# A hybrid decoder layer on one core: the low parts of the weights, the products with g_mix and the cross query's scaling made by VectorE in place of GpSimd

## The chip, the cores and the metric

The kernel runs on one core of a Trainium2 chip. The core has five engines that run side by side: TensorE (PE in the profile; PEld is its loading of the stationary operand), VectorE (DVE), ScalarE (ACT), GpSimd (POOL), and SyncE (SP), which here issues the DMAs. The metric is the device time of one execution in microseconds (us); lower is better.

## The reference

One layer of a decoder for 512 tokens of width 1024, in float32, and a final norm:

```python
h = _rms_norm(x, g_mix[l])
fq, fk, fv, f_logit, dq, dk, dv, gate_a, gate_b = jnp.split(h @ w_in[l], offsets, axis=-1)
...
merged = (jax.nn.sigmoid(gate_a) * (y_a @ w_branch_a[l])
          + jax.nn.sigmoid(gate_b) * (y_b @ w_branch_b[l]))
x = x + merged @ w_out[l]
x = x + _cross_attention(_rms_norm(x, g_cross[l]), _rms_norm(mem, g_mem[l]),
                         w_cq[l], w_ckv[l], w_co[l])
...
x = x + _hier_moe(hm, w_group[l], b_group[l], w_expert[l], b_expert[l],
                  w_exp_gate[l], w_exp_up[l], w_exp_down[l]).reshape(b, s, d)
return _rms_norm(x, g_final)
```

y_a is a causal attention with a forget gate (8 heads of 64), y_b a differential attention with rotary positions (4 heads). The cross-attention has 4 heads and 256 memory rows. The last part routes each token to 2 of 32 experts, whose weights are some 200 MB of float32.

## The kernel before

The program is one long manual schedule: each engine executes its instructions in the order in which the code issues them, and waits where an operand or a buffer is not ready.

**Split products.** The products with the weights of the first half (w_in, the branch, output and cross projections) are made of three matmuls each: every float32 operand is split into a high part, rounded to the fast matmul type, and a low part, the remainder; high x high, low x high and high x low are summed (mm3, L278 to L280). `split` (L175) makes both parts: ScalarE copies the high part (L176), and another engine subtracts it from the source (L177).

**The stream of weights.** A `Stream` object W holds the list of weight chunks in order of use, 32 of them, each 1024 rows by 256 columns or the same size in another shape, and each handled in two halves of 128 x 1024 elements. For a half, SyncE loads the raw weights into one of three buffers (L141), ScalarE makes the high part wh, and the low part wl is made by GpSimd for the halves in the set `self.pool`, that is 12 to 63 without 57 and 59, and by VectorE for the rest. The raw buffer is loaded anew when both parts are done. `W.more()` splits one half ahead; the main loop calls it once per attention iteration behind `it.combine()`, and twice for the second attention (L950 to L956). Outside that loop `W.use` calls it in front of each unit's matmuls.

**The stages.** First x, transposed, is multiplied by g_mix (h_gain, L326; x itself is normed only later, by a factor per token) and split, one tile of 128 tokens at a time, and the first projection is made (to 30 us of the profile). Then 16 iterations of the first attention (class Fox) and 8 of the second (class Diff) follow, each with one or two projection units (t_unit, rope_unit, gate_unit, branch_unit) between the scores and the product with the values; TensorE works through them in this order: scores, unit, values of the iteration before, transposes of the softmax rows (tf or td). VectorE scales the softmax rows (`combine`: L592 for Fox; L698 and L699 for Diff), then evacuates the unit's bank, then copies the transposed rows (pf L603, pd L711). The banks in PSUM are handed out in turn, and the next scores need the banks of the transposed rows. After the attentions come the last units: gate and branch projections, the latter with four instructions of VectorE (L846, L853, two of L857) around two high parts of ScalarE (L856); the keys and values of the memory; and the output projection (out_unit: wop, L1018). The cross query's weights w_cq are multiplied by g_cross when they have been loaded (`self.scale`, L143), before they are split.

**The experts** follow from about 508 us on: per pair of experts TensorE multiplies with 12 pages of 1 MB each, which SyncE loads into a ring of 15 pages as TensorE uses pages up (EX.used).

Of the kernel before, what the change touches and what calls it, by code (L numbers as in the profile page):

```python
# [10 lines left out]
F32 = mybir.dt.float32  # L11
# [4 lines left out]
OP = mybir.AluOpType  # L16
AX = mybir.AxisListType

P = 128
# [3 lines left out]
KD = D // P  # L23
# [15 lines left out]
def tile_hybrid_block(  # L39
# [5 lines left out]
    V, A, PE, G = nc.vector, nc.scalar, nc.tensor, nc.gpsimd  # L45
# [10 lines left out]
    def page(shape, dt, name):  # L56
        return pgp.tile(list(shape), dt, name=name, tag="pg")
# [3 lines left out]
    def work(shape, dt, name, tag="w"):  # L61
        return wk.tile(list(shape), dt, name=name, tag=tag, bufs=bufs[tag])
# [28 lines left out]
    gm = c1.tile([P, KD], F32, name="gm")  # L91
# [14 lines left out]
    def xT(t, k0=0, n=KD):  # L106
        return XT[t // 2][:, t % 2, k0:k0 + n]
# [8 lines left out]
    class Stream:  # L116
        def __init__(self):
            self.spec, self.raw, self.hl = [], {}, {}
            self.loaded = self.done = self.next = 0
            self.lazy = False  # L120
            self.pool = set(range(12, 64)) - {57, 59}
            self.scale, self.new, self.land, self.ahead = {}, {}, {}, {}

        def add(self, src, k, n):
# [3 lines left out]
        def load(self, upto):  # L128

            while self.loaded < min(upto, 2 * len(self.spec), self.done + self.ahead.get(self.loaded // 2, NLD)):  # L130
                i, j = divmod(self.loaded, 2)
                src, k, n = self.spec[i]
                sl = slice(j * k // 2, (j + 1) * k // 2)
                if i in self.land:
                    if j == 0:
                        self.land[i] = page([P, k, n], F32, f"wr{i}")
                    raw = self.land[i][:, sl]
                else:
                    raw = work([P, k // 2, n], F32, f"wr{i}{j}", "ld")
                self.raw[self.loaded] = raw  # L140
                nc.sync.dma_start(raw, src[:, sl])  # L141
                if i in self.scale:
                    G.tensor_tensor(raw, raw, self.scale[i][:, sl, None].to_broadcast([P, k // 2, n]), op=OP.mult)  # L143
                self.loaded += 1

        def split(self, upto):

            while self.done < min(upto, 2 * len(self.spec)):
                i, j = divmod(self.done, 2)
                self.load(self.done + 1)  # L150
                _, k, n = self.spec[i]
                if j == 0:
                    self.hl[i] = [self.new.get((i, u), page)([P, k, n], F32R, f"w{u}{i}") for u in "hl"]
                hi, lo = self.hl[i]
                sl = slice(j * k // 2, (j + 1) * k // 2)
                n = k // 2 // 2 if self.done < 2 else k // 2
                for k0 in range(0, k // 2, n):
                    d = slice(sl.start + k0, sl.start + k0 + n)
                    split(hi[:, d], lo[:, d], self.raw[self.done][:, k0:k0 + n], G if self.done in self.pool else V)
                self.done += 1  # L160
                self.load(self.done + 4)

# [9 lines left out]

            self.split(self.next)

    def split(hi, lo, src, E=V):  # L175
        A.activation(hi, src, AF.Copy)  # L176
        E.tensor_tensor(lo, src, hi.bitcast(F32), op=OP.subtract)  # L177

    W = Stream()

# [114 lines left out]
    def nat_unit(chunk, t, dst, d0, name, nt=1, tag="a"):  # L295

        wh, wl = W.use(chunk, t // 2)
        o = bank(f"{name}p{t}", tag)
        for i in range(nt):
            sl = slice((t + i) * P, (t + i + 1) * P)  # L300
            gemm(o[:, 256 * i:256 * i + 256], KD, lambda k: hk(HH, k, sl), lambda k: hk(HL, k, sl),
                 lambda k: wh[:, k, :], lambda k: wl[:, k, :])

        def evac():
            for i in range(nt):
                A.activation(dst[:, t + i, d0:d0 + 256], o[:, 256 * i:256 * i + 256], AF.Copy, scale=rT[:, t + i:t + i + 1])

        return evac
# [9 lines left out]
    def h_split(t, qs=(0, 1)):  # L318

        sl = slice(t * P, (t + 1) * P)  # L320
        for q in qs:
            split(HH[q][:, :, sl], HL[q][:, :, sl], xT(t, 4 * q, 4))

    def h_gain(t, E, k0=0, n=KD):
        v = xT(t, k0, n)
        E.tensor_tensor(v, v, gm[:, k0:k0 + n, None].to_broadcast([P, n, P]), op=OP.mult)  # L326

    def h_stat(t):
        rms_stat(xt(t), f"nx{t}", out=rT[:, t:t + 1])
# [5 lines left out]

    W.lazy = True
    lg = c1.tile([P, KD, 16], F32R, name="lg")
    h_gain(0, V, 0, 4)
    h_gain(0, G, 4, 4)
    h_split(0, (0,))  # L340
    W.split(1)
    h_split(0, (1,))
    W.split(2)
    evs = []
    for t in range(NT):
        evs.append(nat_unit(c_fv[0], t, fv, 0, "fv0", tag="as"[t // 2]))
        if t + 1 < NT:
            h_gain(t + 1, G)
            h_split(t + 1)
        if t == 1:  # L350
            split(lg[:, :, 0:8], lg[:, :, 8:16], lg_r)
            W.split(3)
        if t == 2:
            h_stat(0)
            h_stat(1)
            evs.pop(0)()
            evs.pop(0)()
            h_stat(2)
            h_stat(3)
# [185 lines left out]
    class Fox:  # L545
# [60 lines left out]
        def av(self):  # L606
            pr, b = self.pr, self.b
            st = Fox.state[pr]
            if b == 0:
                st["y"] = bank(f"yo{pr}", "y")  # L610
            for j in range(b + 1):
                for i in range(2):
                    h = 2 * pr + i
                    PE.matmul(st["y"][64 * i:64 * i + 64, b * P:(b + 1) * P], fv[:, j, h * 64:h * 64 + 64],
                              self.pt[i][:, j * P:(j + 1) * P], start=(b + j == 0), stop=(j == b),
                              skip_group_check=True)
            if b == NT - 1:
                return lambda: lambda: split(YAH[:, pr, :], YAL[:, pr, :], st["y"])
# [690 lines left out]
    for step in """T0 N0 U20 Q0 U21 K0 T1 N1 U30 U22 W Q1 S0 M0 K1 U23 U31 N2 T2 S1 P0 Q2 M1 U32 A0 U33 K2 T3 O0 N3 S2  # L1309
# [5 lines left out]
        f, t = step[0], int(step[1]) if len(step) > 1 else 0  # L1315
# [244 lines left out]
    for p in range(NE // 2):  # L1560
# [4 lines left out]
        for a in range(2):  # L1565
            e = 2 * p + a
            sl = slice((2 * qi + a) * CAP, (2 * qi + a + 1) * CAP)
# [211 lines left out]
```

## Time and profile before

| | |
|---|---|
| median of 3 runs | 1009.11 us (1008.07 to 1009.96) |
| profiled execution | 1009.81 us, its span 1008.1 us |
| PE busy | 966.5 us (96%) |
| DVE busy | 457.2 us (45%) |
| ACT busy | 308.6 us (31%) |
| POOL busy | 200.3 us (20%), of it 120.6 in 50 low parts (L177) |
| granted TensorE clock, mean | 0.984 |

The profile is of one execution. Its time is a little longer than its span, which runs from the first to the last instruction. Times in the rows below count from the start of the span. Line numbers are those of the kernel before; the changed kernel's are one lower from L121 on. A busy TensorE is not one at its peak: matmuls overlap, and their ends are modelled. The granted clock is 1.00 at 2.4 GHz and 0.50 at 1.2 GHz.

### The profile page before, as it was taken

How to read it: one execution, taken by the hardware profiler on the slowest of the kernel's cores; microseconds unless marked ns; L12 is line 12 of the kernel's file. 1: busy time of each engine (PE TensorE's matmuls, PEld its weight loads, DVE VectorE, ACT ScalarE, POOL GpSimd, SP SyncE). 2: the span in 40 equal slices, each digit the busy share in tenths (PEclk: the TensorE clock that was granted, in tenths of full speed). 3: DMA queues.
4: the chain of work that ended last, by engine and by line, in shares of the span. 5: the costliest groups of instructions: out<-in, count | busy, mean ns of one | idle time of the engine just before them, and what ended most of it. 6: DMA issues, size and time to landing. Idle time of an engine off the chain costs nothing. (4 is left out here: it accounts for less than half of the span.)

```text
span 1008.1 us, 13868 instructions
## 1 busy us (share of the span) xinstructions
PE 966.5 (96%) x5494; PEld 643.8 (64%) x5495; DVE 457.2 (45%) x967; ACT 308.6 (31%) x672; POOL 200.3 (20%) x245
## 2 busy tenths in 40 slices
PE   8999899999989999999799999999999999999985
PEld 7787677787878898998646536364453635436332
DVE  6554885846562526445632333323233332233335
ACT  5344444444353344245321112021121212112104
POOL 4841122223444555410100000000000000000003
PEclk8999999999999999999899999999999999999998
DMA  8221121121131247237389899999999999999902
GB/s 307 85 65 62 63 63 64 43 85 63 63 126 63 84 131 266 84 126 301 159 324 422 330 423 416 423 421 418 421 421 422 420 419 421 420 421 419 411 12 84
DMA packets 47862, 246.19 MB, mean 244 GB/s; under 512 B 4784, under 2 KB 12208, under 8 KB 23728
## 3 DMA queue, kind: packets, MB, share of 16 engines
q1 hardware_dynamic: 47648, 245.24, 61.4%
q8 instruction: 45, 0.74, 0.3%
q14 instruction: 25, 0.20, 0.1%
q10 hardware_dynamic: 144, 0.00, 0.0%
HBM read 243.13 MB, written 2.10 MB: 243 GB/s over the span
## 5 line engine op out<-in xcount | busy, mean ns | idle before, releaser
L1410 PE MATMUL gu<-gu,xg 128*64 128x512 f32 x960 | 210.5, 593 | 1.7 <-PEq L1479 1.6
L1410 PEld LDWEIGHTS gu<-gu,xg 128*64 128x64 f32 x960 | 72.9, 137 | 133.2 <-issue 121.1
L177 POOL TENSOR_TENSOR wl<-wr,wh 128x1024 fp32r<-128x1024 f32 x50 | 120.6, 2419 | 186.5 <-ACT wh L176 179.4
L1432 PE MATMUL yd<-dn,A 128*64 128x512 f32 x472 | 110.4, 596 | 0.0
L1454 DVE TENSOR_TENSOR xr<-cb,xr 128x512 f32<-128x512 f32 x120 | 75.7, 684 | 50.6 <-PE cb L1450 50.4
L1415 DVE SCALAR_TENSOR_TENSOR A<-A,gu 128x256 f32<-128x256 f32 x32 | 13.5, 421 | 176.1 <-ACT A L1414 176.1
L1550 POOL MEMSET A<- 128x128 f32 x1 | 0.2, 206 | 438.2 <-PE pth L275 438.2
L1432 PEld LDWEIGHTS yd<-dn,A 128*64 128x64 f32 x472 | 34.9, 137 | 64.3 <-issue 63.4
L1414 ACT ACTIVATE A<-gu 128x256 f32<-128x256 f32 x32 | 12.3, 385 | 201.2 <-PE gu L1410 201.2
L176 ACT ACTIVATE wh<-wr 128x1024 fp32r<-128x1024 f32 (+1 forms) x66 | 67.1, 1026 | 8.0 <-POOL wr L143 6.8
L1450 PE MATMUL cb<-Y,ohT 128*128 128x512 f32 x240 | 67.5, 412 | 0.9
L1440 DVE SCALAR_TENSOR_TENSOR Y<-yd,ws,Y 128x512 fp32r<-128x512 f32 x32 | 23.9, 750 | 91.8 <-ACT Y L1439 89.9
L1238 PE MATMUL ga<-G,hnh 128*128 128x256 f32 x256 | 64.6, 290 | 0.2 <-DVE ge L1358 0.2
L1238 PE MATMUL ga<-G,hnl 128*128 128x256 f32 x256 | 62.8, 283 | 0.0
L1439 ACT ACTIVATE Y<-yd,ws 128x512 fp32r<-128x512 f32 x32 | 21.9, 687 | 126.8 <-PE yd L1432 126.8
L1450 PEld LDWEIGHTS cb<-Y,ohT 128*128 128x128 f32 x240 | 42.7, 191 | 12.5 <-DVE xr L1454 3.2
L1238 PEld LDWEIGHTS ga<-G,hnh 128*128 128x128 f32 x256 | 48.5, 190 | 3.1 <-issue 2.4
L1238 PEld LDWEIGHTS ga<-G,hnl 128*128 128x128 f32 x256 | 48.6, 190 | 0.6
L1384 ACT ACTIVATE xg<-ga,smc 128x256 f32<-128x256 f32 x64 | 29.8, 475 | 52.3 <-PE ga L1238 52.3
L278 PE MATMUL wop<-wh,mh 128*128 128x256 f32 x128 | 36.9, 288 | 2.9 <-DVE xr L1018 1.8
L279 PE MATMUL wop<-wl,mh 128*128 128x256 f32 x128 | 36.4, 284 | 0.6 <-POOL wl L177 0.6
L280 PE MATMUL wop<-wh,ml 128*128 128x256 f32 x128 | 36.3, 283 | 0.0
(611 smaller groups left out, 1962.6 us busy)
## 6 DMA issues: line engine op xcount, KB each, us to landing
gu<-in_w_gu_dram SPq DMA_DIRECT2D x120, 1024.0 KB, 12.3
dn<-in_w_dn_dram SPq DMA_DIRECT2D x55, 1024.0 KB, 17.4
wr<-in_w_inp_dram SPq DMA_DIRECT2D x40, 512.0 KB, 3.7
Z<-in_w_gu_dram SPq DMA_DIRECT2D x8, 1024.0 KB, 14.8
wr<-in_w_out_dram SPq DMA_DIRECT2D x8, 512.0 KB, 6.5
Z<-in_w_dn_dram SPq DMA_DIRECT2D x4, 1024.0 KB, 19.8
dn<-in_w_dn_dram SPq DMA_DIRECT2D x6, 512.0 KB, 13.8
x<-in_x_dram SPq DMA_DIRECT2D x2, 1024.0 KB, 11.6
```

The costliest lines, as they stand in the source:

```text
L176: A.activation(hi, src, AF.Copy)
L177: E.tensor_tensor(lo, src, hi.bitcast(F32), op=OP.subtract)
L278: PE.matmul(o, lh, rh, start=first, stop=False)
L279: PE.matmul(o, lh, rl, start=False, stop=False)
L280: PE.matmul(o, ll, rh, start=False, stop=last)
L1238: PE.matmul(o, CX[u, t // 2][:, t % 2, kb * P:(kb + 1) * P], GQ[q][:, t].rearrange("p e s -> p (e s)"), start=(first and u == "h"), stop=( ...
L1384: A.activation(XG[q][:, kb], o, AF.Copy, scale=gfc[:, kb:kb + 1])
L1410: PE.matmul(gu[64 * f:64 * f + 64, :], xg(2 * i + j), w[:, :, j, 256 * f:256 * f + 256], start=(i + j == 0), stop=(i + j == 4))
L1432: PE.matmul(y[j][64 * a:64 * a + 64, :], hT[a][:, f % 2, f // 2], w(a, f)[:, j, f % 2], start=(f == 0), stop=(f == 3))
L1440: V.scalar_tensor_tensor(yl[rows, j], y[j][rows], ws, yh[rows, j].bitcast(F32), op0=OP.mult, op1=OP.subtract)
L1450: PE.matmul(banks[j], oh[:, t * P:(t + 1) * P], y[u][:, j], start=(u == 0), stop=(u == 1))
L1454: V.tensor_tensor(xs, banks[j], xs, op=OP.add)
```

## The change

GpSimd makes no low part any more, and no product of x with g_mix, and does not scale the cross query's weights; VectorE does, at the same places of the code. One line moves: the product of the second half of the first token tile, which GpSimd made beside the first half's, now stands behind the first half chunk's split, so that VectorE takes it up there.

```diff
-            self.pool = set(range(12, 64)) - {57, 59}
...
                 if i in self.scale:
-                    G.tensor_tensor(raw, raw, self.scale[i][:, sl, None].to_broadcast([P, k // 2, n]), op=OP.mult)
+                    V.tensor_tensor(raw, raw, self.scale[i][:, sl, None].to_broadcast([P, k // 2, n]), op=OP.mult)
...
-                    split(hi[:, d], lo[:, d], self.raw[self.done][:, k0:k0 + n], G if self.done in self.pool else V)
+                    split(hi[:, d], lo[:, d], self.raw[self.done][:, k0:k0 + n])
...
-    def split(hi, lo, src, E=V):
+    def split(hi, lo, src):
         A.activation(hi, src, AF.Copy)
-        E.tensor_tensor(lo, src, hi.bitcast(F32), op=OP.subtract)
+        V.tensor_tensor(lo, src, hi.bitcast(F32), op=OP.subtract)
...
-    def h_gain(t, E, k0=0, n=KD):
+    def h_gain(t, k0=0, n=KD):
         v = xT(t, k0, n)
-        E.tensor_tensor(v, v, gm[:, k0:k0 + n, None].to_broadcast([P, n, P]), op=OP.mult)
+        V.tensor_tensor(v, v, gm[:, k0:k0 + n, None].to_broadcast([P, n, P]), op=OP.mult)
...
-    h_gain(0, V, 0, 4)
-    h_gain(0, G, 4, 4)
+    h_gain(0, 0, 4)
     h_split(0, (0,))
     W.split(1)
+    h_gain(0, 4, 4)
     h_split(0, (1,))
...
-            h_gain(t + 1, G)
+            h_gain(t + 1)
```

VectorE's order at the start, before. xT is x transposed, hh and hl its high and low parts, wl the low part of a weight half, lg the forget gate's weights:

```order
L326 TENSOR_TENSOR xT_83<-xT_83,gm 128x512
L177 TENSOR_TENSOR hl_115<-xT_83,hh_113 128x4x128
L177 TENSOR_TENSOR wl_139<-wr_86,wh_138 128x512 x2
L177 TENSOR_TENSOR hl_116<-xT_83,hh_114 128x4x128
L177 TENSOR_TENSOR wl_139<-wr_89,wh_138 128x512 x2
L177 TENSOR_TENSOR hl_115<-xT_83,hh_113 128x4x128
L177 TENSOR_TENSOR hl_116<-xT_83,hh_114 128x4x128
L177 TENSOR_TENSOR hl_115<-xT_84,hh_113 128x4x128
L177 TENSOR_TENSOR hl_116<-xT_84,hh_114 128x4x128
```

The same place now:

```order
L325 TENSOR_TENSOR xT_83<-xT_83,gm 128x512
L176 TENSOR_TENSOR hl_115<-xT_83,hh_113 128x4x128
L176 TENSOR_TENSOR wl_138<-wr_86,wh_137 128x512 x2
L325 TENSOR_TENSOR xT_83<-xT_83,gm 128x512
L176 TENSOR_TENSOR hl_116<-xT_83,hh_114 128x4x128
L176 TENSOR_TENSOR wl_138<-wr_89,wh_137 128x512 x2
L325 TENSOR_TENSOR xT_83<-xT_83,gm 128x1024
L176 TENSOR_TENSOR hl_115<-xT_83,hh_113 128x4x128
L176 TENSOR_TENSOR hl_116<-xT_83,hh_114 128x4x128
L325 TENSOR_TENSOR xT_84<-xT_84,gm 128x1024
L176 TENSOR_TENSOR hl_115<-xT_84,hh_113 128x4x128
L176 TENSOR_TENSOR hl_116<-xT_84,hh_114 128x4x128
```

The products (gm) stand in the row between the low parts that they feed.

VectorE's order in an iteration of the first attention, before. S are the softmax rows, dqk0l the low part of a unit's result dq0p, pf the copy of the transposed rows, L575 the next iteration's scores:

```order
L592 TENSOR_SCALAR S_1158<-S_1158,ri_1203 128x384
L592 TENSOR_SCALAR S_1159<-S_1159,ri_1203 128x384
L177 TENSOR_TENSOR dqk0l<-dq0p_1172,dqk0h 128x512
L642 TENSOR_TENSOR r000a<-dq0p_1172,rot 128x512
L603 COPY pf_1225<-tf_1213 128x384
L575 ISA S_1239,mx_1241<-sf_1229,cb_967 128x512
```

The same place now:

```order
L591 TENSOR_SCALAR S_1158<-S_1158,ri_1203 128x384
L591 TENSOR_SCALAR S_1159<-S_1159,ri_1203 128x384
L176 TENSOR_TENSOR wl_1208<-wr_947,wh_1207 128x1024
L176 TENSOR_TENSOR dqk0l<-dq0p_1172,dqk0h 128x512
L641 TENSOR_TENSOR r000a<-dq0p_1172,rot 128x512
L602 COPY pf_1225<-tf_1213 128x384
L574 ISA S_1239,mx_1241<-sf_1229,cb_967 128x512
```

The low part of the weights stands behind the scaling of the softmax rows and ahead of the evacuation.

VectorE's order in the output projection, before. xr is x with the sum added to it, wop a unit's bank:

```order
L177 TENSOR_TENSOR wl_3941<-wr_3768,wh_3940 128x1024
L1018 TENSOR_TENSOR xr_3758<-wop_3947,xr_3758 128x256
L1018 TENSOR_TENSOR xr_3758<-wop_3973,xr_3758 128x256
L177 TENSOR_TENSOR wl_4000<-wr_3855,wh_3999 128x1024
L1018 TENSOR_TENSOR xr_3758<-wop_4010,xr_3758 128x256
L1018 TENSOR_TENSOR xr_3758<-wop_4036,xr_3758 128x256
```

The same place now; L142 is the scaling of the cross query's weights:

```order
L176 TENSOR_TENSOR wl_3941<-wr_3768,wh_3940 128x1024 x2
L1017 TENSOR_TENSOR xr_3758<-wop_3947,xr_3758 128x256
L1017 TENSOR_TENSOR xr_3758<-wop_3973,xr_3758 128x256
L176 TENSOR_TENSOR wl_4000<-wr_3855,wh_3999 128x1024
L142 TENSOR_TENSOR wr_4003<-wr_4003,sma 128x1024
L176 TENSOR_TENSOR wl_4000<-wr_3855,wh_3999 128x1024
L142 TENSOR_TENSOR wr_4003<-wr_4003,sma 128x1024
L1017 TENSOR_TENSOR xr_3758<-wop_4010,xr_3758 128x256
L1017 TENSOR_TENSOR xr_3758<-wop_4036,xr_3758 128x256
```

Between two pairs of additions into xr there are now two low parts and the two scalings.

## Rows read from the trace of the kernel before

**Rows 1.** Two stretches, the first attention's and one of the experts': from and to in us, its length, busy us of each engine (x instructions), granted clock, share of the DMA engines, GB/s.

```profile
100.00:195.00 95.00, 89.67 (x574) 69.62 (x571) 71.42 (x150) 41.43 (x88) 24.65 (x11) 1.00 0.19 62
...
700.00:800.00 100.00, 99.74 (x522) 50.70 (x519) 32.80 (x59) 17.27 (x37) 0.00 (x0) 1.00 1.01 421
```

**Rows 2.** Waits of TensorE's weight loads for an expert page from 510 us on: us in total, times, longest.

```profile
PEld gu L1410 <- DMA gu<-in_w_gu_dram: 4.0, 14, 0.3
```

**Rows 3.** Waits of TensorE from 25 to 500 us, the longest of them: us in total, times, longest.

```profile
PE tf L275 <- DVE S L592: 4.6, 6, 1.5
```

**Rows 4.** Timeline of VectorE and GpSimd in the first attention: start, us, engine, line, operation, output and inputs, shapes, count, and in brackets the idle time before and what ended it.

```profile
72.55 0.75 DVE L592 TENSOR_SCALAR S<-S,ri 128x384 f32<-128x384 f32 x2
73.30 1.22 DVE L177 TENSOR_TENSOR wl<-wr,wh 128x1024 fp32r<-128x1024 f32 x1
...
109.17 2.86 DVE L592 TENSOR_SCALAR S<-S,ri 128x384 f32<-128x384 f32 x2
...
109.36 2.44 POOL L177 TENSOR_TENSOR wl<-wr,wh 128x1024 fp32r<-128x1024 f32 x1 [9.28 <-ACT wh L176]
...
153.37 0.88 DVE L592 TENSOR_SCALAR S<-S,ri 128x512 f32<-128x512 f32 x2
...
154.16 2.38 POOL L177 TENSOR_TENSOR wl<-wr,wh 128x1024 fp32r<-128x1024 f32 x1 [6.19 <-ACT wh L176]
```

**Rows 5.** Waits of TensorE from 105 to 195 us, all of them.

```profile
PE tf L275 <- DVE S L592: 3.1, 5, 1.1
PE sd L543 <- ACT pf L603: 0.2, 1, 0.2
```

**Rows 6.** Timeline of TensorE in the second attention, around the transposes td.

```profile
243.94 0.39 PE L279 MATMUL br<-yal,wh 128*128 128x512 f32 x1
244.17 0.39 PE L280 MATMUL br<-yah,wl 128*128 128x512 f32 x1
245.50 0.63 PE L275 MATMUL td<-identf,T 128*128 128x128 f32 x4 [0.94 <-DVE T L699]
246.68 0.63 PE L275 MATMUL td<-identf,T 128*128 128x128 f32 x4 [0.56 <-DVE T L699]
...
247.98 0.88 PE L543 MATMUL sd<-dqk1h 64*128 64x128 f32 x2 [0.19 <-ACT pd L711]
```

**Rows 7.** Timeline of VectorE at the same place.

```profile
242.42 2.93 DVE L699 SCALAR_TENSOR_TENSOR T<-T,dr,T 128x512 f32<-128x512 f32 x1
...
245.78 0.75 DVE L699 SCALAR_TENSOR_TENSOR T<-T,dr,T 128x512 f32<-128x512 f32 x1
...
247.65 0.68 DVE L711 COPY pd<-td 128x512 f32<-128x512 f32 x1
```

**Rows 8.** Three stretches of the second attention, columns as in rows 1.

```profile
244.60:248.00 3.40, 1.75 (x15) 1.26 (x15) 3.37 (x6) 0.59 (x1) 0.21 (x1) 1.00 0.49 154
248.00:254.80 6.80, 6.80 (x25) 5.54 (x26) 4.68 (x17) 2.20 (x9) 0.00 (x0) 0.51 0.01 2
...
298.00:302.00 4.00, 2.23 (x13) 1.55 (x14) 3.60 (x7) 1.95 (x3) 0.33 (x1) 1.00 0.72 266
```

**Rows 9.** Waits of TensorE from 388 to 418 us, all of them.

```profile
PE wop L278 <- DVE xr L1018: 1.8, 2, 1.7
PE wop L278 <- ACT mh L856: 0.6, 1, 0.6
PE wop L279 <- POOL wl L177: 0.6, 1, 0.6
PE wop L278 <- DVE g L846: 0.5, 1, 0.5
```

**Rows 10.** Timeline of VectorE in the branch projections and the output projection, and of GpSimd's scaling of the cross query's weights.

```profile
346.02 0.68 DVE L846 SCALAR_TENSOR_TENSOR g<-g,br 128x512 f32<-128x512 f32 x1
346.73 0.69 DVE L853 TENSOR_TENSOR g<-g,g 128x512 f32<-128x512 f32 x1
347.91 0.76 DVE L857 SCALAR_TENSOR_TENSOR ml<-g,mh 128x256 fp32r<-128x256 f32 x2 [0.48 <-ACT mh L856]
...
392.15 2.85 DVE L853 TENSOR_TENSOR g<-g,g 128x512 f32<-128x512 f32 x1
...
404.08 6.80 DVE L177 TENSOR_TENSOR wl<-wr,wh 128x1024 fp32r<-128x1024 f32 x1
...
406.06 3.74 POOL L143 TENSOR_TENSOR wr<-wr,sma 128x1024 f32<-128x1024 f32 x2
```

**Rows 11.** Timeline of the start.

```profile
3.58 0.69 DVE L326 TENSOR_TENSOR xT<-xT,gm 128x512 f32<-128x512 f32 x1 [2.20 <-DMA gm<-in_small_g_dram]
...
9.71 6.84 POOL L326 TENSOR_TENSOR xT<-xT,gm 128x1024 f32<-128x1024 f32 x3 [1.51 <-DMA xT<-in_x_t_dram]
...
12.55 0.58 PE L279 MATMUL fv0p<-wl,hh 128*128 128x256 f32 x1 [1.33 <-DVE wl L177]
...
16.58 1.15 ACT L176 ACTIVATE hh<-xT 128x512 fp32r<-128x512 f32 x2
...
27.05 0.28 DVE L249 TENSOR_TENSOR rT<-nx_r,nx_t 128x1 f32<-128x1 f32 x1
...
29.04 1.05 PE L370 MATMUL pR<-identf,rT 128*128 128x128 f32 x8
```

**Rows 12.** One stretch of the start, columns as in rows 1.

```profile
12.00:19.00 7.00, 6.01 (x26) 5.72 (x27) 6.85 (x7) 5.75 (x11) 5.80 (x5) 0.54 1.04 406
```

## The prediction

> **What bounds the kernel now.** I read the busy shares by stage first, because the span has two halves with different limits. From 700 to 800 us TensorE is busy 99.74 of 100 us and the DMA engines are full, and GpSimd does nothing [rows 1]; TensorE's waits for an expert page sum to 4.0 us, none over 0.3 us [rows 2]. Nothing of the change runs there. The expert stage therefore takes a fixed time from wherever it starts, and its page loads are issued as TensorE uses up pages (EX.used), so they move with it. The change is worth what it does to the moment at which the first half ends.
>
> In the first half TensorE is also nearly always busy, 89.67 of 95 us in the attention stage [rows 1]. What it loses it loses in short waits for VectorE: 4.6 us for the scaled softmax rows of the first attention (L592) [rows 3], and the like in the second (L699). The third thing to see is why VectorE is late. The pair of L592 took 0.75 us at 72.55, where the low part behind it ran on VectorE, and 2.86 us at 109.17, where GpSimd's low part ran from 109.36 for 2.44 us. At 153.37 the pair took 0.88 us and GpSimd began at 154.16, as it ended [rows 4]. So a VectorE instruction that reads and writes SBUF stands still while GpSimd works on such tiles.
>
> **Attention, 105 to 195 us.** Removed: the lengthening, 2.86 - 0.75 = 2.1 us for each half tile of weights. Added: the same half on VectorE, 1.22 us [rows 4], queued between L592 and the evacuations. VectorE's path is 0.9 us shorter per iteration, and L592's result is ready 2.1 us earlier, because the low part now stands behind it. TensorE's five waits there, 3.1 us in all, longest 1.1 [rows 5], are all shorter than 2.1 us and go. Each wait also costs the overlap of two matmuls: L279 and L280 start 0.23 us apart though each lasts 0.39 [rows 6], so 0.16 us more, five times. Gain 3.1 + 0.8 = 3.9 us. The wait of 1.5 us (4.6 - 3.1) at 102 us is behind rotary tables that VectorE takes from PSUM, and stays. Bounds: what comes late next is the evacuation behind the added 1.22 us, and VectorE is then nearly as long as TensorE in an iteration of 8 to 9 us, so 2.0 at least, and no loss, since VectorE's path gets shorter in each; 5.0 if small delays around the waits go too. I take 3.9.
>
> **Second attention.** At 242.42 L699 took 2.93 us, against 0.75 for the same shape [rows 7]. TensorE then waited 0.94 and 0.56 us for the two transposes and 0.19 us for the copies behind them [rows 6]. The transposes' waits go, but the copy of VectorE (L711, 247.65 [rows 7]) frees the bank that the next scores need, and it now stands behind the low part: it comes 2.93 - 0.75 - 1.22 = 0.96 us earlier, no more. TensorE's wait moves there; gain 0.96 us. The same sequence runs again at 295 us: another 0.96. Together 1.9, bounds 0 (all of it lost behind the low part) and 3.7 (two such places at 0.94 + 0.56 + 0.19 + 0.16).
>
> **The clock.** TensorE was busy 1.75 of the 3.4 us from 244.6, and from 248.0 to 254.8 its granted clock was 0.51, the lower level, 1.2 GHz; from 298 to 302 it was busy 2.23 of 4 us and the clock stayed at 1.00 [rows 8]. At half speed 6.8 us of work cost 3.4 us extra. With the waits at 245 cut from 1.7 to about 0.8 us I expect the clock to stay up: gain 3.4, bounds 0 and 3.4, and I take 3.4 because the shares in the two rows lie close to each other and the new one lies above both.
>
> **The last branch projections and the output projection.** In the four units from 332 us VectorE needs four instructions per unit, and a low part comes to every second one; L853 at 346.73 took 0.69 us, its lengthened form at 392.15 2.85 [rows 10]. A unit is 12 matmuls at 0.23 us, 2.7. VectorE's chain per unit is 0.68 + 0.69 + 0.48 of waiting for the high parts + 0.76 = 2.6 [rows 10], and a low part, 1.22, with the high part that it waits for, about 1.1 by the pair of halves at 16.58 [rows 11], adds 2.3 to every second one. Counted from the first unit's start, VectorE has freed the third unit's bank at 11.1 to 11.4 us, and TensorE wants it for the fifth at 10.9. Loss 0.4, bounds 0 and 1.4. From 388 to 418 us TensorE waited 1.8 + 0.6 + 0.6 + 0.5 = 3.5 us, with five overlaps 4.3 us [rows 9]. The long causes, L853 at 392.15 and the low part of 6.80 us at 404.08 that stood still while GpSimd scaled the cross query's rows for 3.74 us [rows 10], go. New there: six low parts and the two scalings on VectorE, 8 x 1.22 = 9.8 us in 30. The scalings wait for their DMA; behind them are queued the additions into x (L1018) that free TensorE's banks. The load is issued when the last unit's low parts (L857) have freed a page, and VectorE comes to the scaling only behind three more low parts and two output units of TensorE, so I cost that wait at nothing; were it late, this stage's gain would go with it. By the order of instructions the second unit waits 1.6 us for its bank, the third 0.8, none later: 2.4 lost instead of 4.3. Gain 1.9, bounds 0 and 4.3.
>
> **The start.** The products with g_mix leave GpSimd, where three took 6.84 us, for VectorE. A half takes 0.69 there [rows 11], a whole I take as a low part, 1.22. VectorE's low parts lose their lengthening and the fourth quarter of the weights, for which TensorE waited 1.33 us at 12.55 [rows 11], is ready about 1 us earlier. Each product now stands between low parts, though. From 7.9 us, when the second quarter is done, VectorE has a half product, the wait for its high part and three low parts, to 11.0; then a product of 1.2 and, for the high part and two low parts, 1.9, to 14.1; the same again to 17.2; 1.7 for the low parts of the forget gate's and the next weights; and the last product to 20.1. Its high parts, which ended at 17.73 [rows 11], end near 21.2, and the statistics behind them on ScalarE, whose last result came at 27.33, come near 30.1. TensorE reaches pR at 29.04 now and near 28.5 then (last low part 21.9, then 24 matmuls of 256 columns at half of 0.23 and 16 of 512 at 0.23). I count a loss of 0.7, bounds -3.4 (a gain: no stretch at clock 0.54 as from 12 to 19 us [rows 12]) and +4.1 (a new such stretch behind the wait for pR).
>
> **The sum.** 3.9 + 1.9 + 3.4 - 0.4 + 1.9 - 0.7 = 10.0 us. The profiled execution took 1009.81 us, its span 1008.1; that gives 999.8. The median of the runs is 1009.11, 0.7 lower, so I forecast 999.1. SyncE's queue, which waits for a low part before it reloads the raw buffer, is not later: on VectorE the low part stands behind at most the pair L592 of 0.9 us and takes 1.22, together less than GpSimd's 2.44 [rows 4].
>
> **Rivals.**
> The clock does not follow. Everything else happens, but a stretch at 1.2 GHz stays at 248 us or comes at 28 us in its place: 3.4 less, 1002.5; both, 1005.9. For it: the stretch from 244.6 was no idler than the one from 298 [rows 8], so which one trips is partly chance.
>
> The waits change places. L592 is early, but the evacuations behind the added 1.22 us are what TensorE really needs. Then the gains in the attention and the output stage are 0 and only the clock's or a wait's worth is left: 1007 to 1009, say 1008. Against it: TensorE's wait for the copies there is 0.2 us now [rows 5], and VectorE's path gets shorter, not longer.
>
> VectorE becomes the bound, the slower side. If GpSimd was not what lengthened L592, nothing is removed and 11 x 1.22 = 13.4 us are added to 71.42 busy of 95 in the attention stage [rows 1], 85 with ScalarE's waits in between; the eight rotary iterations then cost TensorE about 1.2 us more each, 10 us, and the start and the branch units 1.1: 1020. It decides if L592 stays above 2 us. Against it stands 153.37 [rows 4]. The Trainium skill (Perfetto Trace Analysis, Optimizing Scalar/DVE Operations) says that with VectorE saturated, moving some of its work to GpSimd may pay, which would speak against taking it back, and adds that it might not help since the two share an SBUF port; by its first half the time would be this rival's, by its second the forecast's, and [rows 4] bear out the second.
>
> All waits go and the start keeps full clock: the upper bounds, 5.0 + 3.7 + 3.4 + 4.3 + 3.4 = 19.8, 989.
>
> **How the numbers follow.** The forecast 0.50, the clock 0.27, the waits in other places 0.10, VectorE as bound 0.08, the upper case 0.05. About 0.2%, 2 us, is what a measurement of this kernel can tell from no change. The first, second and last are faster: 0.82; the third is the same, 0.10; the fourth slower, 0.08. The range holds the forecast, both cases of the clock, half of the upper case and half of the third: 993.5 to 1008. The forecast's own range is 996 to 1003.
>
> **What would show it.** L592's pair under 0.9 us everywhere; no wait of tf for it but the one at 102; the pd copy near 246.7 minus the gain so far, with the clock at 1.00 behind it; L853 at 0.7; the scalings of the cross query about 1.2 us with no idle time for their DMA; pR waiting for rT near 29. Wrong: L592 still long, waits of TensorE for evacuations or banks in the attention, or an expert stage that gets longer because its pages come no earlier.

## The result, and the profile after

| | before | after |
|---|---|---|
| median of 8 runs | 1008.46 us (1005.18 to 1010.37) | 1002.37 us (998.48 to 1004.44) |
| ratio, 95% interval | | 0.9933 (0.9913 to 0.9953) |
| profiled execution, span | 1009.81, 1008.1 us | 1002.39, 1000.7 us |
| VectorE busy; GpSimd busy | 457.2; 200.3 us | 473.9; 74.7 us |
| mean granted clock of the profiled execution | 0.984 | 0.990 |

The change is 6.1 us faster by the medians, 7.4 us by the two profiled executions; 10.0 were forecast, to 999.1 us. The sign is right and the time lies in the range; the size is not, and where the missing 3 to 4 us went is what the second attention below and most of the experiments are about.

First the stretches that answer to [rows 1, 8, 12] (from and to, length, busy us of each engine (x instructions), granted clock, DMA share, GB/s):

```profile
12.00:19.00 7.00, 5.95 (x45) 5.34 (x45) 5.41 (x8) 3.40 (x6) 1.26 (x1) 1.00 1.03 402
...
244.60:248.00 3.40, 3.40 (x23) 2.85 (x22) 1.94 (x10) 2.20 (x9) 0.00 (x0) 1.00 0.34 133
...
295.00:298.40 3.40, 3.40 (x9) 2.68 (x10) 1.57 (x2) 0.01 (x1) 0.00 (x0) 0.53 0.58 199
100.00:195.00 95.00, 92.37 (x606) 73.60 (x606) 69.86 (x170) 44.06 (x98) 0.00 (x0) 1.00 0.20 62
...
700.00:800.00 100.00, 99.87 (x529) 50.13 (x530) 30.85 (x57) 16.36 (x34) 0.00 (x0) 1.00 1.01 420
```

In the attention TensorE is busy 92.37 us of 95 where it was 89.67, and VectorE is busy less, 69.86 for 71.42, though it has eleven low parts of half tiles more to make. The expert stage is as it was. Of the clock: the stretches of low clock at 12 us and at 248 us are gone in this execution, and one that was not there before stands at 295.

The waits of TensorE from 105 to 195 us (us in total, times, longest), to be held against [rows 5]:

```profile
PE tf L274 <- DVE S L591: 0.4, 1, 0.4
PE sf L542 <- DVE pf L602: 0.3, 1, 0.3
PE sd L542 <- ACT pf L602: 0.2, 1, 0.2
```

And VectorE's pair at the place where [rows 4] had 2.86 us:

```profile
110.49 0.75 DVE L591 TENSOR_SCALAR S<-S,ri 128x384 f32<-128x384 f32 x2
111.16 1.22 DVE L176 TENSOR_TENSOR wl<-wr,wh 128x1024 fp32r<-128x1024 f32 x1
```

The pair takes 0.75 us, the low part behind it 1.22. Four of five waits for the softmax rows are gone, the fifth is 0.4 us, and one of 0.3 us for VectorE's copy (pf) is new.

The second attention, 195 to 320 us, is where the forecast and the trace part. TensorE's waits there, first before, then after:

```profile
PE td L275 <- DVE T L699: 3.0, 4, 1.0
PE br L278 <- DVE g L846: 0.5, 1, 0.5
PE tz L745 <- DVE g L846: 0.5, 1, 0.5
PE w10p L278 <- DVE g L829: 0.3, 1, 0.3
PE sd L543 <- ACT pd L711: 0.2, 1, 0.2
```

```profile
PE sd L542 <- DVE pd L710: 1.9, 3, 1.2
PE tz L744 <- DVE g L845: 1.6, 1, 1.6
PE br L277 <- DVE g L845: 0.5, 1, 0.5
PE w10p L277 <- DVE g L828: 0.3, 1, 0.3
PE sd L542 <- ACT pd L710: 0.2, 1, 0.2
```

Both lists sum to 4.5 us. The four waits for the transposes (td) are gone, and in their place TensorE waits for VectorE's copies (pd) and for the bank that the evacuation g frees for tz. VectorE's order says why (timeline, columns as in [rows 4]):

```profile
240.53 0.75 DVE L698 SCALAR_TENSOR_TENSOR T<-T,dr,T 128x512 f32<-128x512 f32 x1
241.20 0.68 DVE L735 TENSOR_TENSOR zn<-zo,rq_z 128x512 f32<-128x512 f32 x1
241.80 1.22 DVE L176 TENSOR_TENSOR wl<-wr,wh 128x1024 fp32r<-128x1024 f32 x1
242.93 0.68 DVE L845 SCALAR_TENSOR_TENSOR g<-g,br 128x512 f32<-128x512 f32 x1
243.53 0.68 DVE L710 COPY pd<-td 128x512 f32<-128x512 f32 x1
```

L698 is no longer stretched, but the low part stands between it and both g and pd, back to back with them; the same five stand at 290.49 to 293.49.

From 380 to 412 us, in the output units, TensorE has two waits where [rows 9] had five, and the scaling of the cross query's weights takes 1.22 us on VectorE, with no idle time ahead of it:

```profile
PE wop L277 <- DVE g L845: 1.4, 1, 1.4
PE wop L277 <- DVE xr L1017: 0.5, 1, 0.5
```

```profile
398.65 1.22 DVE L176 TENSOR_TENSOR wl<-wr,wh 128x1024 fp32r<-128x1024 f32 x1
399.78 1.22 DVE L142 TENSOR_TENSOR wr<-wr,sma 128x1024 f32<-128x1024 f32 x1
```

At the start the last matmuls of pR, which followed one another from 29.04 us in [rows 11], now wait for the statistics:

```profile
29.88 0.49 PE L369 MATMUL pR<-identf,rT 128*128 128x128 f32 x2 [0.92 <-DVE rT L248]
```

**The ledger.** TensorE executes the same matmuls in all kernels here, so a matmul's start in one trace less its start in the trace of before says how much has been won or lost up to there. This table, worked out from the traces, has these shifts (us, negative is earlier) at matmuls that stood at the given times before:

| kernel | 30 | 105 | 210 | 312 | 390 | 412 | 515 | 1000 |
|---|---|---|---|---|---|---|---|---|
| after | 0.27 | 0.21 | -3.75 | -5.31 | -4.85 | -7.57 | -7.59 | -7.42 |
| e1_low | 0.36 | 0.30 | -3.91 | -3.87 | -3.40 | -6.13 | -6.11 | -6.33 |
| e2_rest | -0.02 | -0.09 | -0.13 | 0.01 | 0.00 | -1.35 | -1.58 | -1.39 |
| e3_twice | 0.19 | 0.08 | 12.14 | 10.63 | 11.17 | 8.43 | 7.63 | 6.37 |
| e4_copy | 0.01 | -0.02 | 0.50 | -0.98 | -0.48 | -3.21 | -3.20 | -3.11 |
| e5_att | -0.45 | -0.48 | -4.70 | -3.30 | -3.31 | -3.15 | -4.42 | -4.11 |
| e6_diff | 0.27 | 0.23 | 0.23 | -1.34 | -1.35 | -1.01 | -1.96 | -1.77 |
| e7_tail | -1.02 | -1.05 | -1.06 | -2.47 | -2.00 | -4.75 | -5.67 | -5.66 |
| b_all | -0.94 | -1.00 | -4.92 | -11.72 | -11.22 | -16.00 | -16.98 | -16.52 |
| b_diff | 0.36 | 0.29 | -3.58 | -10.43 | -9.93 | -12.64 | -13.59 | -13.16 |
| c_copies | 0.00 | -0.12 | -4.01 | -10.76 | -10.27 | -12.99 | -13.52 | -14.73 |
| b_all_G | -1.16 | -1.19 | -1.15 | -3.57 | -2.69 | -3.81 | -4.35 | -5.81 |
| c_best | -0.89 | -0.92 | -4.81 | -11.66 | -11.16 | -15.93 | -17.13 | -18.50 |

One trace is one execution: where a kernel is not changed (e7_tail at 30 us and from 210 to 312), the shift still moves by 1.0 and 1.4 us, because the stretches of low clock fall differently. That is also what spreads the times. Beside the experiments the kernel before ran 79 times, not counting one execution of 1214.16 us at a mean clock of 0.749: its mean granted clock went from 0.982 to 0.994, and the 15 executions at 0.982 and 0.983 took 1011.6 us in the mean, the 10 at 0.992 to 0.994 1005.1. A line through the 79 has 0.62 us for 0.001 of mean clock. By it, as an estimate, the 8 runs after (1001.95 us and 0.990 in the mean) owe 2.1 of the 7.0 us that they lie below the mean of the 79 (1009.0 us, 0.987) to the clock, and 5.0 to the shorter waits.

### The profile page after: what moved, and what is told of

It is laid out like the page before. It is cut to its first block, busy times and chain, and to the rows that moved or that the text cites. A ratio compares the mean times of both kernels' runs of the same rounds, so it can differ in the third digit from the quotient of the medians.

```text
span 1000.7 us, 13844 instructions
## 1 busy us (share of the span) xinstructions
PE 960.4 (96%) x5494; PEld 639.7 (64%) x5495; DVE 473.9 (47%) x1023; ACT 308.7 (31%) x672; POOL 74.7 (7%) x189
## 5 line engine op out<-in xcount | busy, mean ns | idle before, releaser
L176 DVE TENSOR_TENSOR wl<-wr,wh 128x1024 fp32r<-128x1024 f32 (+1 forms) x66 | 78.4, 1196 | 32.2 <-ACT wh L175 31.6
```

The source lines that it names most:

```text
L176: V.tensor_tensor(lo, src, hi.bitcast(F32), op=OP.subtract)
```

## The experiments

Their kernels start from before or after, as each says. Medians are given with the median of the kernel before on the same chip and the ratio with its 95% interval.

### e1_low and e2_rest: which part of the change

e1_low takes the kernel before and empties the set of halves for GpSimd:

```diff
-            self.pool = set(range(12, 64)) - {57, 59}
+            self.pool = set()
```

> The kernel before with one part of the change: all low parts of the weights on VectorE; the products with g_mix and the scaling of the cross query's rows stay on GpSimd. Theory (the collisions of the low parts carry the gain): the attention's 3.9 us and the second attention's 1.9 us come as in the changed kernel, the output stage less since GpSimd's two scalings still stop VectorE there, the start as before: 1003 to 1004.5 us beside 1008.5 before and 1002.4 with the whole change. Rival (the start and the scalings carry half of it): 1005.5 us or more.

e2_rest takes the kernel after and gives those low parts back to GpSimd (the set and the argument E of split as before).

> The complement: products with g_mix and the scaling on VectorE, the low parts on GpSimd as before. Theory: the scaled softmax rows stay at 2.9 us a pair and the attention waits as before; only the 6.80 us low part of the output stage goes, and the start's saved clock is lost again behind the statistics: 1006.5 to 1008.5 us. Rival (start and scalings carry half): 1005.5 us or less.

Measured: e1_low 1002.45 us beside 1009.41, 0.993 (0.991 to 0.995), the whole of the change's gain and 0.6 below the range that I gave. Its 12 executions had a mean clock of 0.987, that of the kernel before, so this gain is not the clock's. e2_rest 1006.88, 0.998 (0.9961 to 1.0). In e2_rest the attention is as before:

```profile
PE tf L275 <- DVE S L592: 3.1, 5, 1.1
PE sd L543 <- ACT pf L603: 0.2, 1, 0.2
```

So the low parts carry the gain. The ledger says the same by place: e2_rest wins nothing until 390 us and 1.4 at the output; e1_low wins 2.7 at the output, as much as the whole change, so the scalings add nothing once the low parts are on VectorE. I had expected GpSimd's scalings to stop VectorE in e1_low; they took 4.62 us from 395.79, but VectorE's low part that had begun at 395.59 took 1.22 us as ever, and only a pair at 400.09 was a little longer, 2.54 us beside 2.35 at 405.85. At the start all three end within 0.4 us of before. The clock of 1.00 from 12 to 19 us, which the kernel after and e2_rest show, is worth nothing by 30 us: in the kernel after TensorE waits for a high part (1.1 us) and for the statistics (0.9) in its place. In e7_tail, whose start is that of before, the same clock is worth 1.0 us by 30 us; so at like clock the start's new order costs about 1.3 us.

### e3_twice and e4_copy: is it the collision?

Both take the kernel after and let GpSimd work for halves 14 to 23 on a tile that nobody reads; VectorE's own work is that of the kernel after.

```diff
                     split(hi[:, d], lo[:, d], self.raw[self.done][:, k0:k0 + n])
+                    if 14 <= self.done < 24:
+                        G.tensor_tensor(scr, self.raw[self.done], hi[:, d].bitcast(F32), op=OP.subtract)
...
+    scr = c1.tile([P, 4, 256], F32, name="scr")
```

In e4_copy the line of GpSimd is `G.tensor_copy(scr, hi[:, d].bitcast(F32))`.

> The changed kernel, in which GpSimd makes ten low parts of the attention (halves 14 to 23) a second time, into a tile that nobody reads. Theory (GpSimd's work on SBUF tiles stops VectorE): the pairs of L592 in 105 to 195 us take 2.5 to 2.9 us again though VectorE's own work is unchanged, the low part behind them comes later too, and TensorE loses at least the 3.9 us again: 1006 to 1012 us, and in the profile the shift against the kernel before is gone by 195 us. Rival (the gain came from the order on VectorE or from the low part's earlier end, not from the collision): pairs under 0.9 us and 1002.4 us.

> As the run before it, but GpSimd copies the high part into the tile (one operand read in place of two). Theory in its wide form (any GpSimd instruction on SBUF tiles stops VectorE): the pairs of L592 take as much longer as the copy lasts behind their start, over 1.5 us, and the time is 1004 to 1010 us. Rival (only instructions with two operands collide): pairs under 0.9 us, 1002.4 us.

Measured: e3_twice 1016.19 us, 1.0078 (1.0045 to 1.0112), slower than before; e4_copy 1005.61, 0.9971 (0.9953 to 0.999). The timeline of VectorE and GpSimd, first e3_twice, then e4_copy:

```profile
120.62 3.06 DVE L594 TENSOR_SCALAR S<-S,ri 128x512 f32<-128x512 f32 x2
...
120.87 2.52 POOL L160 TENSOR_TENSOR scr<-wr,wh 128x1024 f32<-128x1024 f32 x1 [7.84 <-ACT wh L177]
...
123.60 1.21 DVE L178 TENSOR_TENSOR wl<-wr,wh 128x1024 fp32r<-128x1024 f32 x1
```

```profile
110.28 1.53 DVE L594 TENSOR_SCALAR S<-S,ri 128x384 f32<-128x384 f32 x2
...
110.46 1.14 POOL L160 COPY scr<-wh 128x1024 f32<-128x1024 f32 x1 [48.46 <-ACT wh L177]
```

The pair (L594 in these kernels) takes 3.06 us in the one, at 128x512, where [rows 4] have 0.88 for that shape, and 1.53 in the other, at 128x384, beside 0.75. It ends 0.3 and 0.2 us behind GpSimd's instruction in each: 120.87 + 2.52 = 123.39 and 123.68; 111.60 and 111.81. The rival, that order or an earlier low part was what helped, is out: order and place on VectorE did not change, only GpSimd's work came back. The wide form holds: a copy with one operand stops VectorE too. The price was larger than I expected. In e3_twice the shift goes from -3.75 to +12.14 at 210 us. TensorE's waits from 105 to 210 us are now not only for the rows, but for VectorE's copies behind them:

```profile
PE tf L277 <- DVE S L594: 5.7, 7, 1.8
PE sd L545 <- DVE pf L605: 1.3, 1, 1.3
PE sf L545 <- DVE pf L605: 1.3, 1, 1.3
...
```

and the clock falls, twice for 3.4 us (at 113 and 127 us) and once for 6.8:

```profile
113.40:116.80 3.40, 3.40 (x14) 2.21 (x15) 3.40 (x7) 0.48 (x1) 0.00 (x0) 0.53 0.33 114
127.00:130.40 3.40, 3.40 (x13) 2.68 (x12) 2.22 (x8) 1.30 (x5) 0.00 (x0) 0.54 0.19 74
202.10:208.90 6.80, 5.52 (x28) 5.10 (x28) 4.64 (x14) 2.85 (x10) 0.00 (x0) 0.52 0.26 77
```

At half clock these cost up to (3.4 + 3.4 + 6.8) / 2 = 6.8 us of the 15.9. This run has both the collision and the low part on VectorE, which is what the prediction priced as "VectorE becomes the bound", at some 10 us in this stage; measured are 12.1 against before, up to 6.8 of them the clock, which that price did not contain.

### e5_att, e6_diff, e7_tail: what each stage is worth

The kernel before with VectorE making the low parts of one stage alone: the set of halves for GpSimd is cut to 24 to 63 (e5_att), to 12 to 23 and 40 to 63 (e6_diff, as shown), and to 12 to 39 (e7_tail, where VectorE also scales the cross query's rows).

```diff
-            self.pool = set(range(12, 64)) - {57, 59}
+            self.pool = set(range(12, 64)) - set(range(24, 40)) - {57, 59}
```

> The kernel before, with VectorE making the low parts of halves 12 to 23 alone (89 to 195 us). Theory (each stage's collisions have their own worth, as the steps add them): TensorE is 3.9 us earlier at 195 us and gains nothing more behind it, pairs of L592 under 0.9 us: 1004.5 to 1006 us beside some 1009 before. Rival (the waits change places): shift at 195 us under 1 us, 1008 us or more.

> The kernel before, with VectorE making the low parts of halves 24 to 39 alone (199 to 318 us, the second attention). Theory without the clock: 1.9 us earlier behind the two places at 245 and 298 us, 1006.5 to 1007.5 us. Theory with the clock as forecast (no stretch at 1.2 GHz behind either place): 5.3 us, 1003 to 1004.5 us. Third: the transposes no longer wait but the next scores do, as long as before: 1008.5 us or more.

> The kernel before, with VectorE making the low parts from half 40 on and scaling the cross query's rows. By the forecast's terms 1.9 - 0.4 = 1.5 us earlier at 412 us, by the changed kernel's trace 2.7: 1006 to 1007.5 us. Rival (VectorE, loaded with six more low parts, costs TensorE as much in the branch and output units as the collisions did): 1008.5 us or more.

Measured beside 1009.3: e5_att 1004.06 us, 0.9948 (0.9927 to 0.9968); e6_diff 1007.03, 0.9981 (0.9964 to 0.9997); e7_tail 1005.87, 0.9967 (0.9948 to 0.9987). The attention is worth 4.2 us in its own stage (-0.48 to -4.70), the output units 2.8 (-2.00 to -4.75). Three such parts add up to more than the whole (0.0104 against 0.0067); with intervals of 0.002 on each I leave that open. By the ledger the stages that are changed agree with e1_low: 4.2 us from 105 to 210 in e5_att and in e1_low, 2.3 from 312 to 412 in e7_tail and in e1_low; what e7_tail has beyond that came where nothing was changed. e6_diff is the one that tells. Its waits from 195 to 320 us are those of the kernel after to the tenth:

```profile
PE sd L543 <- DVE pd L711: 1.9, 3, 1.2
PE tz L745 <- DVE g L846: 1.6, 1, 1.6
...
```

and its 1.6 us from 210 to 312 have a stretch of low clock behind them that is half as long as the 6.8 us of [rows 8] (here 3.4 us at 248.5), worth 1.7. Without the clock nothing is won there in this execution: the third of the cases that I had put on record for it. That the median, 1007.03, lies in the range of the first case is the clock's luck: over the 12 executions (1007.14 us and 0.9887 in the mean) the line through the mean clocks gives 1.2 of the 1.9 us to it. e1_low agrees: its low clock in this stage, twice 3.4 us at 245 and 297, is as long as that of before, and its shift there does not move, -3.91 to -3.87.

### b_all: three orders altered

From here on the kernels start from after. b_all alters the order at the three places where TensorE still waits for VectorE: at the start W.pre makes the high part where it was and W.split(3) the low part only behind the last product; in the second attention the copies and the low part move; in the last four branch units the low part is made while VectorE waits for mh.

```diff
             split(lg[:, :, 0:8], lg[:, :, 8:16], lg_r)
+            W.pre()
+        if t == 2:
             W.split(3)
-        if t == 2:
             h_stat(0)
...
-                (V.tensor_copy if i == 0 else A.copy)(r[:, 0:self.n], self.tb[i][:, 0:self.n])
+                A.copy(r[:, 0:self.n], self.tb[i][:, 0:self.n])
...
                 A.activation(MH[i][:, 4 * c + j], ga[:, sl], AF.Copy, scale=0.5)
+            if W.hook is not None:
+                W.split(W.hook)
...
-        W.more()
-        if isinstance(it, Diff):
+        if isinstance(it, Fox):
+            W.more()
+        else:
             ev()
             while late:
                 late.pop(0)()
+            W.more()
             ev = unit()
...
```

> The changed kernel with three orders altered: at the start VectorE makes the low part of the next weights behind the last product with g_mix and its low parts, not ahead; in the second attention both copies of the transposed rows go to ScalarE and the low part of the weights stands behind the evacuation of the first unit; in the last four branch units the low part is made between the sum g and its low parts, while VectorE waits for ScalarE, with its high part made ahead. Theory (what TensorE still waits for there is VectorE's order): 1.2 us at the start, twice 1.0 and once 1.2 in the second attention, 2.0 at the output: some 6 us less than the changed kernel, 995 to 998 us. Rival (the waits only move to the next instruction of VectorE or ScalarE): 1001 to 1004 us.

Measured: 992.91 us beside 1009.3, 0.9842 (0.9819 to 0.9866), 9.5 below the kernel after and below what I expected. By the ledger the start gives 1.2 us, the output 2.1, both as expected, and the second attention 5.2 (6.80 from 210 to 312 in place of 1.56), where I had 3.2; 1.7 of the 5.2 are the low clock at 295 us (half of 3.4), which b_all does not have.

### b_diff and c_copies: what TensorE waits for in the second attention

b_diff has the second attention's two orders of b_all alone, c_copies only the one line that gives both copies to ScalarE.

> The changed kernel with the second attention's two orders alone: both copies of the transposed rows on ScalarE, the low part of the weights behind the first unit's evacuation. Theory (from 210 to 312 us VectorE is what TensorE waits for, so the change gave nothing there but clock): of 5.6 us that TensorE loses in these waits some 3.5 come back, 1.7 more if no stretch at 1.2 GHz stays: 997 to 999.5 us. Rival (the stretch of low clock was the loss, and waits of under 2 us there cost nothing on balance): 1001 to 1002.5 us.

> As the run before, but only the copies go to ScalarE; the low part stays ahead of the evacuations. Theory: the next scores' waits for the copies (3.2 us lost in five places from 233 to 283 us) fall to about 1, the wait for the bank of the transposed values at 293 us (1.7) stays: 1000 to 1001 us. Rival (the low part ahead of the evacuation is the one cause): 1002 us or more, the waits moving to the evacuation.

Measured beside 1009.19: b_diff 996.79 us, 0.9875 (0.985 to 0.9901), just under the range that I gave; c_copies 994.88, 0.9863 (0.9835 to 0.9891). The copies do it all; moving the low part as well adds nothing that can be told apart. TensorE's waits in c_copies from 195 to 320 us, ScalarE's two copies at 240.87, and the stretch from 210 to 307 us:

```profile
PE tz L744 <- DVE g L845: 1.6, 1, 1.6
PE w10p L277 <- DVE g L828: 0.3, 1, 0.3
```

```profile
240.87 1.07 ACT L710 COPY pd<-td 128x512 f32<-128x512 f32 x2 [2.45 <-PE td L274]
```

```profile
210.00:307.00 97.00, 94.92 (x533) 78.50 (x532) 60.97 (x125) 46.56 (x122) 16.46 (x56) 1.00 0.27 87
```

ScalarE had been idle for 2.45 us and makes both copies in 1.07. No wait for pd is in the list any more, the wait of tz for g stays as expected, and the clock is 1.00 throughout. I had expected 1000 to 1001 us. By the ledger 7.3 us lie between the two profiled executions: 5.2 in this stage, of them 1.7 the clock that I hadn't counted, and 1.9 behind 412 us, where the kernels are the same and the clock fell differently (the kernel after has 3.4 us at half clock at 957 us, c_copies has none there).

### b_all_G: is the change still worth it with the better orders?

b_all with the set of halves for GpSimd restored (`E` of split as before).

> All three altered orders, but the low parts from half 12 on (without 57 and 59) on GpSimd, as in the kernel before. Theory (the collisions are a cost of their own beside VectorE's order): the attention's 4 us are lost again, and the places where GpSimd's low part now falls on the scaled rows or on the sums of the branches lose their 1 to 2 us: 998 to 1003 us. Rival (the orders alone carry the gain, and with them GpSimd's help is worth having): 994 us or less.

Measured: 1003.99 us, 0.995 (0.9931 to 0.9969), 1 us above the upper end that I gave, and 11.1 above b_all. The waits for the stopped instructions are back, tf 4.5 us in six waits from 100 to 200 us, and from 195 to 320 us:

```profile
PE td L290 <- DVE T L715: 3.1, 4, 1.0
PE tz L761 <- DVE g L862: 0.5, 1, 0.5
...
```

These are the four td waits of before. The collision costs 11 us with the better orders, almost twice what it cost with the old ones, where VectorE's queue in the second attention took back what its end gave. The clock has a part in the 11: b_all_G ran twice for 3.4 us at half clock, at 296 and at 392 us, where b_all did not, and that cost up to 3.4 us.

### c_best

The kernel after with b_all's start and output orders and the copies of c_copies, the low part left where the change has it.

> The changed kernel with what the runs so far showed to pay: VectorE's and ScalarE's orders of the start and of the last four branch units as in the run with three orders, both copies of the transposed rows on ScalarE, and the low part of the weights left where the change has it. By the table of TensorE's shifts: the copies alone stand at 994.9 us, the start is worth 1.0 and the output 2.0 more: 991.5 to 993 us, and below the run with three orders by at most 0.5. Rival (the gains overlap, since earlier arrivals only wait at the next place): 994 us or more.

Measured: 991.91 us beside 1009.56, 0.9839 (0.9815 to 0.9864), as expected. It is not to be told from b_all (992.91); both are the fastest, some 17 us below before and 10 below after. TensorE's only wait for VectorE from 370 to 412 us is

```profile
PE wop L292 <- DVE xr L1044: 0.2, 1, 0.2
```

## Why the prediction was right or wrong

**Why GpSimd costs time: right, and shown.** The pair took 0.75 us, e3_twice brought 3.06 back by GpSimd's work alone, and e1_low has the whole gain. The rival in which VectorE becomes the bound fell with the 0.75.

**Attention, 3.9 us: right, in part by luck.** 3.96 in the kernel after (0.21 to -3.75), 4.2 in e5_att. The waits in the list fell by 2.4 us (3.3 to 0.9): one of 0.4 us stayed that I had let go, and one of 0.3 came. The other 1.6 us, overlap and delays that the list does not show, I had at 0.8.

**Branch units, -0.4, and start, -0.7: right in kind.** The fifth unit waits 0.4 us for its bank, and the shift goes from -5.31 to -4.85 there. The start loses 0.3; the full clock behind 12 us, which I had only as a bound, came and was lost again, in part at pR, whose wait I had foreseen near 29. The small loss hides two terms, about 1.3 lost by the order and 1.0 given back by that clock (e7_tail).

**Output projection, 1.9 us: 2.7.** The two waits foreseen at 1.6 and 0.8 measured 1.4 and 0.5. Of the edits there the scalings were worth 1.4 us alone (e2_rest) and nothing beside the low parts (e1_low).

**Second attention, 1.9 us, and the clock, 3.4: here the sum failed.** Together 5.3 were forecast; the kernel after has 1.56 from 210 to 312 us. I had written "TensorE's wait moves there; gain 0.96 us" for the copy at 245, and "the same sequence runs again". The wait did move to the copy, 1.2 us of it at 244, but VectorE's copies were late in two more iterations as well (0.15 us at 233, 0.55 at 254), and at 293 us it was the bank behind g, not the copy, that came late, by 1.6. I had followed VectorE's order at one place and multiplied, where in five of the stage's eight iterations a low part stands directly ahead of a copy or of the evacuation in front of it (231.28, 241.80, 252.32, 281.26 and 291.76 us). The waits of the stage sum to 4.5 us before and after: the term of 1.9 us came out at nothing, since the shorter low clock accounts for all of the 1.56 us. The rival "the waits change places", which I had priced for the attention and the output, is what happened in this stage.

The clock's step leaned on two rows of which I called the first no idler than the second; 1.75 of 3.4 us is 51% busy and 2.23 of 4 is 56%. "With the waits at 245 cut from 1.7 to about 0.8 us I expect the clock to stay up", held for that place in this execution, and a new stretch came at 295, behind the waits of 1.6 and 0.5 us there. It was not the shorter wait that decided it: e6_diff, with the same waits to the tenth, has its 3.4 us of low clock at 248 and none behind the waits of 1.6 and 0.5 us, which end at 299 and 300 us there, and e1_low, with nearly the same, has 3.4 us at each. In this execution the clock's worth in the stage is (6.8 - 3.4) / 2 = 1.7, not 3.4. Over the runs it is 2.1 by the line through the mean clocks. The rival "the clock does not follow" had 1002.5 us and a chance of 0.27, and the median is 1002.37; yet its mechanism, a stretch that stays at 248 or comes at 28, is not what this profile shows, though e6_diff and e1_low show the first half of it.

What c_copies adds is the reason: from 210 to 312 us TensorE waits for what VectorE queues ahead of the copies. Taking the collision away made room on VectorE, and the low part used it up.

## What to carry to other kernels

Before an instruction is given to GpSimd, look at what VectorE does in the same microseconds: in these traces VectorE's instructions from SBUF to SBUF that TensorE waited for (L592, L699) stood still until GpSimd's ended, with VectorE busy 45% of the span. When a low part, a copy or any filler moves onto an engine, read that engine's whole order in each iteration, and ask what stands behind the filler; a copy that an engine idle at that moment could make (ScalarE here) was worth another 7.5 us by the medians, some 3.6 of the 7.3 in the ledger being the clock. And do not book the clock's gain in full: with the same waits the low clock stood at 295 us in one kernel here and at 248 in another.

## What the runs showed of the hardware

GpSimd's copy with one operand stops VectorE as its subtraction with two does, each until about 0.2 to 0.3 us past its own end (111.60 and 111.81; 123.39 and 123.68). The Trainium skill (SBUF — State Buffer, section "SBUF: two separate sides") describes the pair of ports that VectorE and GpSimd share as a lock held for a whole instruction, not a bandwidth that is split; the traces agree, with pairs of L594 at 3.06 us beside 0.88 and at 1.53 beside 0.75.

One kernel, unchanged, took from 1004.3 to 1012.8 us in 79 executions, and the longer times came, in the mean, with the lower of its granted clocks, 0.982 to 0.994. In the kernel after the clock fell to 0.53 at 295 us behind two waits of 1.6 and 0.5 us, and in e3_twice at 113 us behind waits of under 2 us; in c_copies, with one wait of 1.6 us that ended at 290.31, it did not, and in e6_diff it did not fall there behind the same two waits. What decides between them is not settled by these runs.
